# Seven-product down projections over both column halves, kept in two PSUM banks

## The chip, the cores and the metric

The kernel runs on one core of a Trainium2 chip. The metric is the device time of one execution in microseconds, the median of several runs. The engines are named PE or TensorE (matmuls), ACT or ScalarE, DVE or VectorE, POOL or GpSimd, and SP, whose queue only issues transfers here.

## The reference, cut to what matters

A decoder trunk of two layers works on 256 tokens of width 2048 in float32. Each layer adds a mixer to the residual (layer 0: windowed attention and a state-space scan, layer 1: dilated attention) and then an MLP. The change touches the MLPs alone, with D_FF = 8192:

```
def squared_relu_mlp(h, w_up, w_down):
    u = jnp.einsum('bsd,df->bsf', h, w_up)
    return jnp.einsum('bsf,fd->bsd', jnp.square(jax.nn.relu(u)), w_down)
...
        h = rms_norm(x, norm_ffn[layer])
        x = x + squared_relu_mlp(h, w_up[layer], w_down[layer])
```

## The kernel before, in words

Products are made with split numbers: every float32 operand becomes a high part (hi, a copy by ScalarE to float32r) and a low part (lo, the difference, by VectorE). A product of two such operands is three matmuls: hi x hi, hi x lo and lo x hi.

All matmul work stands in one list, `plan` (line 219 on), of pieces. A piece covers two k-tiles of 128 rows (KC = 2) and 512 weight columns, so one weight tile of 128x1024 and 512 KB. A piece of a `Unit` makes 12 matmuls: 2 k-tiles x 2 token halves x 3. `run` (line 270) walks the list and, while it issues piece i, runs ahead of it: the weight load of piece i + 6 on SP's queue (`fetch`), the hi copy of piece i + 3 (`high`, ScalarE), the lo subtraction of piece i + 2 (`low`, VectorE), and any weight sum of piece i + 4 (`add`, VectorE). The buffers are 4 loaded tiles (wraw), 5 of hi and 4 of lo. Each engine works through its instructions in the order in which they were issued.

Work beside the matmuls (norms, attention, activations, splits) is written as generators; `side` queues them, and `tick` (line 173), called once per k-tile or once per seven-product piece, lets them issue some steps when ScalarE and VectorE are not too far ahead by an estimate of their load. `need` forces them on until a label is done.

An MLP has 16 up units of 512 columns (8 pieces each) and 8 chunks c of two up results. After an up unit, `squared` (line 929) runs relu, 8 transposes through PSUM (tile uT) and Square. `operands` (line 948) then splits the results of a chunk into uh and ul and, in all chunks but the last, forms four sums of activations s1 and s2 and splits them into sh and sl; it starts when the chunk before has issued all its products. `down` (line 983) is the usual down unit: one chunk's 8 k-tiles times 512 columns, 4 pieces, added to a stripe of the residual `res` by VectorE.

`Seven` (line 243) takes the place of two down units. With tokens in two halves, a chunk's rows in two and the columns in two, the product of a 2x2 block matrix of activations and one of weights needs 7 block products instead of 8 (a scheme after Strassen and Winograd): 7 products x 2 pieces x 6 matmuls = 84 instead of 96. In exchange, sums of weight blocks and of activation blocks are needed. Before the change this is done for column stripes 0 and 1 of chunks 0 to 6 in each layer; stripes 2 and 3 and all of chunk 7 go through `down`. The weight blocks (tile sraw) are 128x1024 tiles in a pool of 29 slots with the tag w4, which many other tiles share; four of the seven weight operands are sums made by VectorE. Each product has a PSUM bank of its own (tile sp, from the four aux banks that transposes use too). `evict` (line 995) adds it to the residual, or, for P1, Q5 and Q6, to running sums in SBUF that `together` (line 1009) combines into the residual once per layer; the first two stripes of chunk 7 wait for that (`pre`).

The order of a chunk: up, two down units, up, with the 14 seven-product pieces spread between them from place 4.5 on.

Of the kernel before, what the change touches and what calls it, by code (L numbers as in the profile page):

```python
# [11 lines left out]
OP = mybir.AluOpType  # L12
# [28 lines left out]
def trunk(ctx: ExitStack, tc: tile.TileContext, x, norm_mix, norm_ffn, w_up, w_down, ab_w_in, ab_q_norm,  # L41
# [193 lines left out]
    def unit(*a, **k):  # L235
# [4 lines left out]
    SEVEN = (("P1", "11", None), ("P2", "21", None), ("Q3", "22", None), ("Q5", "11", "12"), ("Q7", "12", "22"),  # L240
             ("Q6", "11", "22"), ("Q4", "11", "21"))

    class Seven:


        def __init__(self, w, rows, c0, kts, operands, evict, needs, mark):
            self.w, self.rows, self.c0, self.operands, self.evict, self.needs, self.mark = \
                w, rows, c0, operands, evict, needs, mark
            self.halves = kts // KC
            self.raw = {}  # L250
            self.pieces = [(self, (p, h)) for p in range(7) for h in range(self.halves)]

        def fetch(self, p, h):
            _, block, other = SEVEN[p]
            b = block if other is None else "12" if p == 3 else None
            if b is not None:
                r, c = self.rows[int(b[0]) - 1] + h * KC, self.c0 + (int(b[1]) - 1) * W
                self.raw[b, h] = t = work.tile([128, KC, W], F32, name="sraw", tag="w4")
                nc.sync.dma_start(t, self.w[r * 128:(r + KC) * 128, c:c + W].rearrange("(k p) c -> p k c", p=128))

        def add(self, p, h):
            _, block, other = SEVEN[p]
            if other is not None:
                t = self.raw[block, h]
                V.tensor_tensor(t, t, self.raw[other, h], op=OP.add)

        def source(self, p, h):
            return self.raw[SEVEN[p][1], h]

    def run():  # L270
# [32 lines left out]
        def low(i):  # L303
            if i < len(todo):
# [3 lines left out]
                parts[i].append(lo)  # L308

# [15 lines left out]
        before = ps = sp = None  # L325
        kept, held = [], []
        for i, (u, c) in enumerate(todo):
# [9 lines left out]
            if isinstance(u, Seven):  # L337
                p, h = c
                name = SEVEN[p][0]
                if p in u.needs and h == 0:  # L340
                    need(u.needs[p])
                if h == 0:
                    sp = aux("sp")
                xh, xl, t0 = u.operands(name)
                tick(True)
                for k in range(KC):
                    q = h * KC + k
                    wh, wl = xh[:, q, t0:t0 + 128], xl[:, q, t0:t0 + 128]
# [249 lines left out]
    def residual_unit(w, ktiles, j, needs={}, nm=None, last=None, pre=None, mark=None):  # L598
# [557 lines left out]
```

## Time and profile before

| | |
|---|---|
| median of 3 runs | 2298.36 us (2297.48 to 2298.86) |
| the profiled execution's own time | 2297.73 us |
| its span | 2295.9 us |
| granted TensorE clock, mean | 0.998 |
| busy: PE, DVE, ACT | 2277.0, 1692.5, 1239.9 us |
| matmuls of 512 columns in seven-product pieces (sp) | 1176 |
| matmuls of 512 columns in down units (acc on uh, ul) | 1728 |
| weight sums by VectorE (sraw<-sraw) | 112 |
| HBM read | 420.64 MB |

The span is the time from the first to the last instruction of the profiled execution; its own time is that of the whole launch. A busy TensorE says only that a matmul was under way: matmuls overlap, so their pace is read from the starts of neighbouring ones. A group's last figure is the idle time of the engine just before its instructions, with what ended it. "PE acc" is a matmul into an accumulator of a unit, "PE sp" one into a bank of the seven products; whi and wlo are the weights' hi and lo, hThi and hTlo those of the normed input, uh and ul those of the up result, and sh and sl those of its sums.

### The profile page before, as it was taken

What the parts mean: (1) busy time and instruction counts of PE and PEld (TensorE: products, weight loads), DVE (VectorE), ACT (ScalarE), POOL (GpSimd) and SP (SyncE); (2) the same over time, 40 slices, a digit from 0 to 9 for tenths busy, and PEclk for the clock granted to TensorE, in tenths of its full rate; (3) what the DMA queues carried; (4) which work ended last, traced back from release to release, by engine and by line L of the source; (5) the groups of instructions that cost most, each with busy time, mean ns of one, the idle gap of its engine ahead of it and who ended that gap; (6) DMA issues with size and microseconds to landing.
All of it is one profiled execution on the core that took longest, in us unless ns stands there. A gap on an engine that the chain in (4) does not pass through costs nothing.

```text
span 2295.9 us, 29951 instructions
## 1 busy us (share of the span) xinstructions
PE 2277.0 (99%) x11149; PEld 1898.3 (83%) x11149; DVE 1692.5 (74%) x2418; ACT 1239.9 (54%) x1561; POOL 8.4 (0%) x20
## 2 busy tenths in 40 slices
PE   8999999999999999999999999999999999999998
PEld 7998988888888888888788778778888888888887
DVE  6779976556787787787866766665577787787785
ACT  5565554445556556556454555555555555555553
POOL 1000000000000000000000000000000000000000
PEclk9999999999999999999999999999999999999999
DMA  7546565566556656656456455545756656656654
GB/s 232 166 139 193 174 186 173 191 186 222 187 176 223 187 177 222 188 177 222 145 177 190 148 162 160 173 156 178 221 163 217 206 164 217 205 164 218 204 165 145
DMA packets 229202, 424.73 MB, mean 185 GB/s; under 512 B 15620, under 2 KB 26160, under 8 KB 229056
## 3 DMA queue, kind: packets, MB, share of 16 engines
q1 hardware_dynamic: 218976, 416.34, 58.1%
q10 hardware_dynamic: 9568, 6.34, 0.9%
q8 instruction: 87, 1.43, 0.2%
q14 instruction: 59, 0.48, 0.1%
q0 software_dynamic: 512, 0.15, 0.0%
HBM read 420.64 MB, written 2.13 MB: 184 GB/s over the span
## 4 chain that ended last, share of the span: by engine, by line
PE 98%; DVE 1%; DMA 0%; ACT 0%; issue 0%; SPq 0%; ACTq 0%
PE acc L71 81%; PE sp L71 12%; PE uT L71 1%; PE sc L71 1%; PE o L71 1%; PE pT L71 1%; PE yp L71 1%; PE xT L71 1%; DMA wraw<-in_ab_w_in_dram 0%; DVE res L71 0%; PE qp L71 0%; DVE wlo L71 0%; PE yo L71 0%; PE kp L71 0%; PE yT L71 0%; PE xtok L71 0%
## 5 line engine op out<-in xcount | busy, mean ns | idle before, releaser
L71 ACT ACTIVATE whi<-wraw 128x1024 fp32r<-128x1024 f32 (+1 forms) x680 | 717.4, 1056 | 641.4 <-PE acc L71 518.1
L71 DVE TENSOR_TENSOR wlo<-wraw,whi 128x1024 fp32r<-128x1024 f32 (+1 forms) x680 | 823.4, 1216 | 314.7 <-PE acc L71 227.5
L71 PE MATMUL acc<-whi,hThi 128*128 128x512 f32 (+1 forms) x1632 | 645.5, 396 | 2.6 <-ACT hThi L71 2.6
L71 PE MATMUL acc<-whi,hTlo 128*128 128x512 f32 (+1 forms) x1632 | 634.7, 389 | 0.3 <-DVE hTlo L71 0.3
L71 PE MATMUL acc<-wlo,hThi 128*128 128x512 f32 (+1 forms) x1632 | 633.9, 388 | 0.0
L71 PEld LDWEIGHTS acc<-whi,hThi 128*128 128x128 f32 x1632 | 307.6, 189 | 68.1 <-issue 5.9
L71 PEld LDWEIGHTS acc<-whi,hTlo 128*128 128x128 f32 x1632 | 307.3, 188 | 64.7 <-DVE hTlo L71 0.9
L71 PEld LDWEIGHTS acc<-wlo,hThi 128*128 128x128 f32 x1632 | 307.8, 189 | 60.4 <-issue 1.0
L71 ACT ACTIVATE whi<-sraw 128x1024 fp32r<-128x1024 f32 x196 | 207.7, 1060 | 178.4 <-DVE sraw L71 151.1
L71 DVE TENSOR_TENSOR wlo<-sraw,whi 128x1024 fp32r<-128x1024 f32 x196 | 239.7, 1223 | 59.4 <-PE acc L71 30.4
L71 PE MATMUL acc<-whi,uh 128*128 128x512 f32 x576 | 228.7, 397 | 3.4 <-ACT uh L71 3.4
L71 PE MATMUL acc<-whi,ul 128*128 128x512 f32 x576 | 226.0, 392 | 1.7 <-DVE ul L71 1.7
L71 PE MATMUL acc<-wlo,uh 128*128 128x512 f32 x576 | 225.5, 391 | 0.0
L71 DVE TENSOR_TENSOR sraw<-sraw 128x1024 f32<-128x1024 f32 x112 | 136.6, 1220 | 0.0
L71 PEld LDWEIGHTS acc<-whi,ul 128*128 128x128 f32 x576 | 108.9, 189 | 25.7 <-DVE ul L71 2.6
L71 PEld LDWEIGHTS acc<-whi,uh 128*128 128x128 f32 x576 | 108.9, 189 | 25.4 <-ACT uh L71 3.8
L71 PEld LDWEIGHTS acc<-wlo,uh 128*128 128x128 f32 x576 | 109.0, 189 | 21.7
L71 PE MATMUL acc<-hThi,whi 128*128 128x256 f32 x384 | 112.3, 293 | 0.0
L71 PE MATMUL acc<-hThi,wlo 128*128 128x256 f32 x384 | 108.5, 283 | 0.0
L71 PE MATMUL acc<-hTlo,whi 128*128 128x256 f32 x384 | 108.5, 283 | 0.0
L71 PE MATMUL sp<-whi,sh 128*128 128x512 f32 x224 | 87.1, 389 | 0.0
L71 PE MATMUL sp<-wlo,sh 128*128 128x512 f32 x224 | 87.1, 389 | 0.0
(228 smaller groups left out, 2535.9 us busy)
## 6 DMA issues: line engine op xcount, KB each, us to landing
wraw<-in_w_up_dram SPq DMA_DIRECT2D x256, 512.0 KB, 3.7
wraw<-in_w_down_dram SPq DMA_DIRECT2D x144, 512.0 KB, 4.3
sraw<-in_w_down_dram SPq DMA_DIRECT2D x112, 512.0 KB, 5.9
wraw<-in_ab_w_in_dram SPq DMA_DIRECT2D x96, 512.0 KB, 3.7
wraw<-in_c_w_qkv_dram SPq DMA_DIRECT2D x96, 512.0 KB, 4.0
wraw<-in_ab_w_out_dram SPq DMA_DIRECT2D x48, 512.0 KB, 3.7
wraw<-in_c_w_o_dram SPq DMA_DIRECT2D x32, 512.0 KB, 3.7
wt<-cumd ACTq DMA_DIRECT2D x8, 512.0 KB, 6.5
```

The costliest lines, as they stand in the source:

```text
L71: return f(out, *a, **k)
```

## The change

- `Seven` is made for a column offset: `seven(c, j)` for stripes j and j + 1. Chunks 0, 2 and 4 of each layer use it for both halves (j = 0 and j = 2) and have no down units; chunks 1, 3, 5 and 6 use it for stripes 0 and 1 as before. That is 20 sets in place of 14.
- Up units come in another order: 3 in the chunks with both halves, 1 in the chunks 1, 3 and 5, and units 14 and 15 at the head of chunk 6 with the two down units behind them.
- The seven products of a set go to two long-lived PSUM banks (a: P1, Q6, Q5, Q3; c: Q7, Q4) and a third for P2. A bank is not cleared between its products; after each product VectorE adds or subtracts the bank's running sum to or from one block of the residual. The running sums in SBUF, `together` and the wait `pre` are gone.
- Of the four weight sums, one (block 11 + block 12) is made by a transfer issued from GpSimd that reads block 12 from HBM and adds it to the tile of block 11 (`accum_op`); it is issued behind P1's lo subtraction, which reads that tile. The other three stay on VectorE, Q6's with a tile of its own (t2). The three loads of blocks 21, 12 and 22 are issued together with P2.
- The sums of activations have the opposite sign: two of the four operations become scalar_tensor_tensor.
- `operands` waits for all products of the chunk before, and for chunk 7 only for the up result.

```
```diff
@@ -237,35 +237,55 @@
-    SEVEN = (("P1", "11", None), ("P2", "21", None), ("Q3", "22", None), ("Q5", "11", "12"), ("Q7", "12", "22"),
-             ("Q6", "11", "22"), ("Q4", "11", "21"))
+    SEVEN = (("P1", "a", "11"), ("P2", "b", "21"), ("Q6", "a", "t2"), ("Q7", "c", "12"), ("Q5", "a", "11"),
+             ("Q4", "c", "21"), ("Q3", "a", "22"))
+    LOADS = {"P1": ("11",), "P2": ("21", "12", "22")}
+    SUMS = {"Q6": ("t2", "11", "22"), "Q7": ("12", "12", "22"), "Q4": ("21", "21", "t2")}
     class Seven:
-        def __init__(self, w, rows, c0, kts, operands, evict, needs, mark):
-            self.w, self.rows, self.c0, self.operands, self.evict, self.needs, self.mark = \
-                w, rows, c0, operands, evict, needs, mark
+        def __init__(self, w, rows, c0, kts, operands, to, needs, mark):
+            self.w, self.rows, self.c0, self.operands, self.to, self.needs, self.mark = \
+                w, rows, c0, operands, to, needs, mark
             self.halves = kts // KC
-            self.raw = {}
+            self.raw, self.bank = {}, {}
             self.pieces = [(self, (p, h)) for p in range(7) for h in range(self.halves)]
+        def tile(self, b, h):
+            self.raw[b, h] = t = work.tile([128, KC, W], F32, name="sraw", tag="w4")
+            return t
         def fetch(self, p, h):
-            _, block, other = SEVEN[p]
-            b = block if other is None else "12" if p == 3 else None
-            if b is not None:
+            for b in LOADS.get(SEVEN[p][0], ()):
                 r, c = self.rows[int(b[0]) - 1] + h * KC, self.c0 + (int(b[1]) - 1) * W
-                self.raw[b, h] = t = work.tile([128, KC, W], F32, name="sraw", tag="w4")
-                nc.sync.dma_start(t, self.w[r * 128:(r + KC) * 128, c:c + W].rearrange("(k p) c -> p k c", p=128))
+                nc.sync.dma_start(self.tile(b, h),
+                                  self.w[r * 128:(r + KC) * 128, c:c + W].rearrange("(k p) c -> p k c", p=128))
         def add(self, p, h):
-            _, block, other = SEVEN[p]
-            if other is not None:
-                t = self.raw[block, h]
-                V.tensor_tensor(t, t, self.raw[other, h], op=OP.add)
+            if SEVEN[p][0] in SUMS:
+                o, x, y = SUMS[SEVEN[p][0]]
+                x, y = self.raw[x, h], self.raw[y, h]
+                V.tensor_tensor(self.raw[o, h] if o != "t2" else self.tile(o, h), x, y, op=OP.add)
+        def accumulate(self, p, h):
+            if SEVEN[p][0] == "P1":
+                r, c = self.rows[0] + h * KC, self.c0 + W
+                nc.gpsimd.dma_start(self.raw["11", h],
+                                    self.w[r * 128:(r + KC) * 128, c:c + W].rearrange("(k p) c -> p k c", p=128),
+                                    accum_op=OP.add)
         def source(self, p, h):
-            return self.raw[SEVEN[p][1], h]
+            return self.raw[SEVEN[p][2], h]
+        def evict(self, p):
+            name, b, _ = SEVEN[p]
+            t, j, op = {"P1": (0, 0, OP.add), "P2": (0, 0, OP.add), "Q6": (1, 0, OP.add), "Q7": (1, 1, OP.subtract),
+                        "Q5": (1, 1, OP.subtract), "Q4": (1, 0, OP.add), "Q3": (0, 1, OP.subtract)}[name]
+            r = self.to[t][j]
+            V.tensor_tensor(r, r, self.bank[b], op=op)
     def run():
         todo = plan
@@ -306,6 +326,9 @@
                 lo = wpool.tile([128, KC, raw.shape[2]], F32R, name="wlo", bufs=AHEAD + 1)
                 V.tensor_tensor(lo, raw, f32(parts[i][0]), op=OP.subtract)
                 parts[i].append(lo)
+                u, c = todo[i]
+                if isinstance(u, Seven):
+                    u.accumulate(*c)
         for i in range(RAW):
             if i % 2 == 0:
@@ -336,21 +359,23 @@
             hi, lo = parts.pop(i)
             if isinstance(u, Seven):
                 p, h = c
-                name = SEVEN[p][0]
+                name, b, _ = SEVEN[p]
                 if p in u.needs and h == 0:
                     need(u.needs[p])
-                if h == 0:
-                    sp = aux("sp")
+                new = b not in u.bank
+                if new:
+                    u.bank[b] = aux("sp")
+                sp = u.bank[b]
                 xh, xl, t0 = u.operands(name)
                 tick(True)
                 for k in range(KC):
                     q = h * KC + k
                     wh, wl = xh[:, q, t0:t0 + 128], xl[:, q, t0:t0 + 128]
-                    PE.matmul(sp, wh, hi[:, k], start=q == 0, stop=False)
-                    PE.matmul(sp, wh, lo[:, k], start=False, stop=False)
-                    PE.matmul(sp, wl, hi[:, k], start=False, stop=q == u.halves * KC - 1)
+                    PE.matmul(sp, wh, hi[:, k], start=new and k == 0, stop=False, skip_group_check=True)
+                    PE.matmul(sp, wh, lo[:, k], start=False, stop=False, skip_group_check=True)
+                    PE.matmul(sp, wl, hi[:, k], start=False, stop=q == u.halves * KC - 1, skip_group_check=True)
                 if h == u.halves - 1:
-                    pending.append(lambda u=u, name=name, sp=sp: u.evict(name, sp))
+                    pending.append(lambda u=u, p=p: u.evict(p))
                     if p == 6:
                         done.add(u.mark)
                 continue
@@ -947,9 +970,11 @@
         def operands(c):
-            if c:
-                yield from until(("seven", layer, c - 1))
-                yield from until(("rest", layer, c - 1))
+            if 0 < c < NC - 1:
+                for k in marks[c - 1]:
+                    yield from until(k)
+            if c == NC - 1:
+                yield from until(("uf", layer, 2 * c + 1))
             for i in (2 * c, 2 * c + 1):
                 yield from until(("uf", layer, i))
                 u[i] = slot("uh"), slot("ul")
@@ -961,10 +986,10 @@
             a1, a2 = uf[2 * c], uf[2 * c + 1]
             s1, s2 = w4([128, 4, T], "s1"), w4([128, 4, T], "s2")
             o, n = slice(0, 128), slice(128, T)
-            V.tensor_tensor(s1[:, :, o], a1[:, :, n], a2[:, :, n], op=OP.subtract)
-            V.tensor_tensor(s1[:, :, n], a1[:, :, o], s1[:, :, o], op=OP.subtract)
-            V.tensor_tensor(s2[:, :, o], a1[:, :, n], a1[:, :, o], op=OP.subtract)
-            V.tensor_tensor(s2[:, :, n], a2[:, :, o], s1[:, :, n], op=OP.subtract)
+            V.tensor_tensor(s1[:, :, o], a2[:, :, n], a1[:, :, n], op=OP.subtract)
+            V.scalar_tensor_tensor(s1[:, :, n], a1[:, :, o], -1.0, s1[:, :, o], op0=OP.mult, op1=OP.subtract)
+            V.tensor_tensor(s2[:, :, o], a1[:, :, o], a1[:, :, n], op=OP.subtract)
+            V.scalar_tensor_tensor(s2[:, :, n], a2[:, :, o], -1.0, s1[:, :, n], op0=OP.mult, op1=OP.subtract)
             yield 2
             sums[c] = [(slot("sh"), slot("sl")) for _ in range(2)]
             for (h, l), s in zip(sums[c], (s1, s2)):
@@ -980,63 +1005,44 @@
             return Unit([(wu, i * W, W)], nm.ktiles(), lambda ps: after_up(i, ps),
                         needs=nm.needs() if i == 0 else {}).pieces
+        marks = {c: [] for c in range(NC)}
         def down(c, j):
             kts = [(4 * (2 * c + b) + k, (lambda b=b, k=k: u[2 * c + b] + (k,))) for b in range(2) for k in range(4)]
             end = c == NC - 1
+            marks[c].append(("down", layer, c, j))
             return residual_unit(wd, kts, j, {4 * b: ("u", layer, 2 * c + b) for b in range(2)},
-                                 nxt if end else None, last if end else None,
-                                 ("seven's sums", layer) if end and j < 2 else None,
-                                 ("rest", layer, c) if j == NS - 1 else None).pieces
...
-        def seven(c):
+                                 nxt if end else None, last if end else None, marks[c][-1]).pieces
+        def seven(c, j):
             def parts(name):
                 i, k, t = {"P1": (0, 0, 0), "P2": (0, 1, 0), "Q4": (0, 1, 128), "Q5": (1, 0, 0), "Q6": (1, 0, 128),
                            "Q7": (1, 1, 0), "Q3": (1, 1, 128)}[name]
                 return (sums[c][k] if i else u[2 * c + k]) + (t,)
-            return Seven(wd, (8 * c, 8 * c + 4), 0, 4, parts, lambda name, ps: evict(c, name, ps),
+            marks[c].append(("down", layer, c, j))
+            return Seven(wd, (8 * c, 8 * c + 4), j * W, 4, parts,
+                         [[res[:, t, (j + i) * W:(j + i + 1) * W] for i in range(2)] for t in range(2)],
                          {0: ("u", layer, 2 * c), 1: ("u", layer, 2 * c + 1), 2: ("sums", layer, c)},
-                         ("seven", layer, c)).pieces
+                         marks[c][-1]).pieces
+        def mixed(rest, s, start):
+            n, k = len(s), 0
+            for i, x in enumerate(rest):
+                while k < n and i >= start + (len(rest) - start) / n * k:
+                    plan.append(s[k])
+                    k += 1
+                plan.append(x)
+            plan.extend(s[k:])
         plan.extend(up(0) + up(1))
-        for c in range(NC - 1):
-            rest = up(2 * c + 2) + down(c, 2) + down(c, 3) + up(2 * c + 3)
-            s = seven(c)
-            for k, x in enumerate(rest):
-                while s and k >= 4.5 + (len(rest) - 4.5) / 14 * (14 - len(s)):
-                    plan.append(s.pop(0))
-                plan.append(x)
-            plan.extend(s)
+        for c, (ups, both) in enumerate((((2, 3, 4), 1), ((5,), 0), ((6, 7, 8), 1), ((9,), 0), ((10, 11, 12), 1),
+                                         ((13,), 0), ((14, 15), 0))):
+            p = [up(i) for i in ups]
+            d = [] if both else [down(c, 2), down(c, 3)]
+            order = p[:1] + d + p[1:] if c < NC - 2 else p + d
+            mixed(sum(order, []), seven(c, 0) + (seven(c, 2) if both else []), 4.5)
         for j in range(NS):
             plan.extend(down(NC - 1, j))
```

## Rows read from the trace of the kernel before

**Rows 1.** The page, part 1: busy time and share of the span, by engine.
```profile
PE 2277.0 (99%) x11149; PEld 1898.3 (83%) x11149; DVE 1692.5 (74%) x2418; ACT 1239.9 (54%) x1561; POOL 8.4 (0%) x20
```

**Rows 2.** The page, part 4: the chain that ended last, by engine.
```profile
PE 98%; DVE 1%; DMA 0%; ACT 0%; issue 0%; SPq 0%; ACTq 0%
```

**Rows 3.** The chain in order of time: start us, length us, what, matmuls.
```profile
725.83 5.44 PE acc L71 x24
...
812.04 5.44 PE acc L71 x24
```

**Rows 4.** The page, part 5: one group of the seven products' matmuls.
```profile
L71 PE MATMUL sp<-whi,sh 128*128 128x512 f32 x224 | 87.1, 389 | 0.0
```

**Rows 5.** Timeline of TensorE at both layers' ends: start us, us, what, [idle before].
```profile
1136.52 0.39 PE L71 MATMUL acc<-whi,hTlo 128*128 128x512 f32 x1
...
1140.36 0.50 PE L71 MATMUL acc<-whi,uh 128*128 128x512 f32 x1 [1.68 <-ACT uh L71]
...
1143.40 0.63 PE L71 MATMUL acc<-whi,ul 128*128 128x512 f32 x1
1143.83 0.63 PE L71 MATMUL acc<-whi,uh 128*128 128x512 f32 x1
...
1145.09 0.39 PE L71 MATMUL acc<-whi,uh 128*128 128x512 f32 x1
...
2241.86 0.39 PE L71 MATMUL acc<-whi,hTlo 128*128 128x512 f32 x1
...
2251.04 0.39 PE L71 MATMUL acc<-whi,ul 128*128 128x512 f32 x1
```

**Rows 6.** Timeline of ScalarE at the end of layer 0's MLP.
```profile
1136.27 1.37 ACT L71 ACTIVATE relu<-acc,rs 128x512 f32<-128x512 f32 x2 [0.98 <-PE acc L71]
...
1139.24 2.01 ACT L71 ACTIVATE uh<-uf 128x1024 fp32r<-128x1024 f32 x2
```

**Rows 7.** The page, part 5: groups of VectorE (count, busy us, mean ns).
```profile
L71 DVE TENSOR_TENSOR wlo<-sraw,whi 128x1024 fp32r<-128x1024 f32 x196 | 239.7, 1223 | 59.4 <-PE acc L71 30.4 <-issue 24.8
...
L71 DVE TENSOR_TENSOR sraw<-sraw 128x1024 f32<-128x1024 f32 x112 | 136.6, 1220 | 0.0
...
L71 DVE TENSOR_TENSOR res<-sp,res 128x512 f32<-128x512 f32 x56 | 38.6, 690 | 10.8 <-PE sp L71 9.2
```

**Rows 8.** Timeline of VectorE where its operations follow one another.
```profile
845.28 1.22 DVE L71 TENSOR_TENSOR sraw<-sraw 128x1024 f32<-128x1024 f32 x1
846.42 0.69 DVE L71 TENSOR_TENSOR pq<-sp,pq 128x512 f32<-128x512 f32 x1
847.02 1.22 DVE L71 TENSOR_TENSOR wlo<-wraw,whi 128x1024 fp32r<-128x1024 f32 x1
```

**Rows 9.** Stretches: length, busy us by engine, clock, DMA share, GB/s.
```profile
718.00:804.00 86.00, 86.00 (x389) 71.23 (x388) 67.79 (x66) 47.97 (x51) 0.00 (x0) 1.00 0.63 195
798.00:804.00 6.00, 6.00 (x30) 4.99 (x29) 4.06 (x5) 3.64 (x5) 0.00 (x0) 1.00 0.95 323
920.00:940.00 20.00, 20.00 (x90) 16.57 (x89) 18.54 (x19) 10.15 (x10) 0.00 (x0) 1.00 0.46 133
```

**Rows 10.** Timeline of GpSimd: one issue of a 16 KB transfer.
```profile
8.97 0.56 POOL L124 DMA_DIRECT2D dtb<-in_ab_dt_bias_dram  x1
```

**Rows 11.** DMA issues: transfer, queue, count, KB each, median us to landing.
```profile
sraw<-in_w_down_dram SPq DMA_DIRECT2D x112, 512.0 KB, 5.9
...
par<-in_norm_mix_dram ACTq DMA_DIRECT2D x1, 16.0 KB, 2.1
...
dtb<-in_ab_dt_bias_dram POOLq DMA_DIRECT2D x1, 16.0 KB, 5.2
```

**Rows 12.** The tile wraw: landing of its 512 KB loads.
```profile
DMA to landing us min/median/max: 3.4/3.8/9.6
```

**Rows 13.** Waits of VectorE and of SP's queue: us in total, times, longest us.
```profile
DVE wlo L71 <- PE acc L71: 257.9, 186, 3.0
...
SPq L285 <- DVE wlo L71: 1813.0, 629, 7.8
```

More of the change, by code (lines that the diff above doesn't have):

```diff
@@ L324, in run @@
         pending = []
-        before = ps = sp = None
+        before = ps = None
         kept, held = [], []
@@ L596, in add_stripe, with residual_unit @@
         free(ps)
-    def residual_unit(w, ktiles, j, needs={}, nm=None, last=None, pre=None, mark=None):
+    def residual_unit(w, ktiles, j, needs={}, nm=None, last=None, mark=None):
         def after(ps):
-            if pre is not None:
-                need(pre)
             add_stripe(ps, j, last)
@@ L985, in down @@
             end = c == NC - 1
+            marks[c].append(("down", layer, c, j))
             return residual_unit(wd, kts, j, {4 * b: ("u", layer, 2 * c + b) for b in range(2)},
-                                 nxt if end else None, last if end else None,
-                                 ("seven's sums", layer) if end and j < 2 else None,
-                                 ("rest", layer, c) if j == NS - 1 else None).pieces
-        keep = {}
-        R = [[res[:, t, j * W:(j + 1) * W] for j in range(2)] for t in range(2)]
-        def evict(c, name, ps):
-            if c == 0 and name == "P1":
-                keep["pq"], keep["q6"] = w4([128, 2, W], "pq"), w4([128, W], "q6")
-                keep["P1"], keep["Q5"], keep["Q6"] = keep["pq"][:, 0], keep["pq"][:, 1], keep["q6"]
-                V.tensor_tensor(R[1][0], R[1][0], R[1][1], op=OP.add)
-            if name in keep and c == 0:
-                S.activation(keep[name], ps, AF.Copy)
-            else:
-                r = {"P2": R[0][0], "Q3": R[0][1], "Q4": R[1][0], "Q7": R[1][1]}.get(name)
-                r = keep[name] if r is None else r
-                V.tensor_tensor(r, ps, r, op=OP.add)
-            if c == NC - 2 and name == "Q4":
-                side(together(), ("seven's sums", layer))
-        def together():
-            P1, Q5, Q6 = keep["P1"], keep["Q5"], keep["Q6"]
-            V.tensor_tensor(R[0][0], P1, R[0][0], op=OP.add)
-            V.tensor_tensor(P1, Q6, P1, op=OP.subtract)
-            V.tensor_tensor(R[1][1], P1, R[1][1], op=OP.add)
-            V.tensor_tensor(R[1][0], R[1][0], R[1][1], op=OP.subtract)
-            yield 2
-            V.tensor_tensor(P1, P1, Q5, op=OP.add)
-            V.tensor_tensor(R[0][1], P1, R[0][1], op=OP.add)
-            V.tensor_tensor(R[1][1], Q5, R[1][1], op=OP.add)
-            yield 1
-        def seven(c):
+                                 nxt if end else None, last if end else None, marks[c][-1]).pieces
+        def seven(c, j):
             def parts(name):
```

## The prediction, made before the kernel was run

> **What bounds the kernel now.** I read the page's busy table first, then the chain of waits, then TensorE's own timeline where the chain breaks. TensorE is busy 2277.0 of 2295.9 us and carries 98% of the chain that ended last [rows 1, 2], so time is won by taking matmuls away or by closing TensorE's few gaps, and lost where another engine opens new ones. The chain in order of time gives the price of a matmul: 24 of them in 5.44 us, 0.2267 us each [rows 3]; the 389 ns that the groups show [rows 4] is the length of one, and they overlap. The two rows of [rows 3] stand at the same place of two neighbouring chunks, 812.04 - 725.83 = 86.21 us apart. A chunk has 2 x 96 matmuls of up, 2 x 48 of down and 84 of the seven products: 372 x 0.2267 = 84.33 us. The other 1.88 us are its 16 uT transposes, 0.118 us each. So inside the layer TensorE has no gap at all; VectorE and ScalarE wait for it.
>
> The gaps are at the end of each MLP. There the chunk's last up unit is followed at once by the down unit that needs its result: relu, transposes, Square, the split, and then matmuls that first run at half pace [rows 5, 6].
>
> **Part 1, fewer matmuls.** Chunks 0, 2 and 4 of both layers replace two down units (96 matmuls) by one more set of seven products (84). That is 6 sets x 12 = 72 matmuls of 128x512, 72 x 0.2267 = 16.3 us, all on the path, since TensorE sets the pace there. Weight loads go with the matmuls and transposes stay the same. Both bounds of this term are near: TensorE can't gain more than 16.3 here, and what it can lose is in the parts below.
>
> **Part 2, the last up units earlier.** In chunk 6 the order becomes up 14, up 15, down, down, so eight down pieces (8 x 12 x 0.2267 = 21.8 us) and about half of the seven products lie between the end of up 15 and the first matmul of chunk 7. The chain to be hidden is short: from the last up matmul at 1136.52 to the first down matmul at 1140.36 [rows 5, 6]. What it costs today: in layer 0 the tenth down matmul starts at 1145.09, the first after which the pace is 0.23 us again. Without a gap it would start 0.227 us (the last up matmul) + 0.94 us (8 transposes) + 9 x 0.2267 us after 1136.52, at 1139.73: 5.4 us lost. In layer 1 the twelfth starts at 2251.04 and would have started at 2241.86 + 0.23 + 0.94 + 11 x 0.2267 = 2245.52: 5.5 us. The part behind the gap is TensorE's clock: matmuls 0.43 us apart instead of 0.23, after an idle engine; no gap, no slow matmuls. I take the whole 10.9 us. If another 2 us gap took its place, most of the slow stretch would come back with it, and the term would be near 0.
> The final combination (8 additions of VectorE per layer and the wait for them ahead of the first two stripes) goes too. It lies beside this same chain and is not priced again.
>
> **Part 3, what VectorE gets.** Each piece of the seven products needs a hi copy on ScalarE and a lo subtraction on VectorE for only 6 matmuls (1.36 us), where another piece has 12 (2.72 us). VectorE's 128x1024 operations take 1.22 us each, but follow one another every 1.13 to 1.14 us, and the 512-column ones every 0.60 us [rows 7, 8].
> A chunk with both halves: 52 pieces, 12 weight sums, 2 ul, 2 sl, so 68 x 1.14 = 77.5 us, and 14 evictions and 4 sums of activations, 18 x 0.6 = 10.8: 88 us. TensorE takes 456 x 0.2267 + 24 x 0.118 = 106.2 us for it. A chunk with one half: 40 x 1.14 + 15 x 0.6 = 54.6 us against 276 x 0.2267 + 0.94 = 63.5. So 83 and 86%; before, it is 67.8 of 86 us [rows 9]. Locally it is tighter. From Q6 to Q4 in a one-half chunk there are 8 + 5 pieces, 24.5 us of TensorE, with 13 subtractions, 6 sums, 4 evictions and 2 stripes: 19 x 1.14 + 6 x 0.6 = 25.3 us, 0.8 us too much. TensorE always has about three pieces ready, 4 to 7 us, which covers it; the trace already has stretches of 18.5 in 20 us without a gap on TensorE [rows 9]. I cost this at 0; if every operation took its full 1.22 us it would be 2.4 us of backlog, still covered.
> The evictions now go straight into the residual (0.69 us, the same row as before), and a bank's next product comes two pieces after its eviction, so TensorE doesn't wait for it. Two scalar-tensor-tensor operations replace two subtractions in each chunk, at the same size: 0 to 0.06 us each on VectorE (hidden).
>
> **Part 4, the accumulating DMA.** New for the trace: 40 transfers (20 sets x 2) of 512 KB issued by GpSimd, each behind the lo subtraction of P1 on the same tile, each awaited by VectorE's sum for Q6. GpSimd has nothing else to do in this stretch, its issue takes about 0.56 us [rows 10], and SP's queue is not passed. Behind the waiting sum on VectorE stand the lo subtractions of the next pieces, and TensorE waits for those.
> The time there is: lo has 4 buffers, so VectorE does P1's lo when TensorE has finished the piece four places ahead, and Q6's sum comes after the lo two places ahead of it in the same way. Between these two TensorE works through five pieces, which by their order are 9.5 to 12.2 us, in one case four pieces, 8.2 us. If the sum is late, TensorE still has four pieces ready, 6.8 to 8.2 us; less the three 1.14 us operations that VectorE has to do in them, 3.4 to 4.7 us are to spare. So TensorE starves only if issue to landing takes longer than about 13 us (12.9 to 15.6 by place).
> How long it takes is bounded from rows [rows 11, 12]. From below: a 16 KB transfer from GpSimd lands after 5.2 us, one from ACT after 2.1, and the fastest 512 KB load after 3.4, so 5.2 + (3.4 - 2.1) = 6.5 us. From above: twice the slowest 512 KB load and GpSimd's extra 3.1, 2 x 9.6 + 3.1 = 22.3 us. I take 5.2 + (5.9 - 2.1) = 9.0 us, since the median load of the same tile is the nearest row. That is inside the time there is: 0 us.
> At the upper end each set would stall TensorE for 22.3 - 14 = 8.3 us, 20 x 8.3 = 166 us.
> The Trainium skill, Collectives: The Full Stack, section "The bandwidth ceiling: the fold count and why AG ≠ RS ≠ AR", says that an add inside a DMA needs two source reads and so ran at about half the rate of a copy. By that rule the estimate would be 5.2 + 2 x 3.8 = 12.8 us, which still adds nothing to the sum but uses up the margin. No run here shows such a transfer yet.
> Other DMA traffic: three loads of a half are now issued together at P2, six within about 4 to 7 us, with one or two other loads, some 3.7 MB. At the 323 GB/s that a busy stretch moves [rows 9] they take 11 us, and SP runs ahead by four other pieces (about 18 us in the dense part), because its waits are for lo on the other pieces' buffers [rows 13]. In total there are as many loads as before (48 fewer wraw, 48 more sraw) and 21 MB more from the accumulating ones, 5% of 420 MB. Cost 0; without SP's lead, ScalarE would wait 1 to 3 us in each set.
>
> **Sum.** 2297.73 (the profiled execution's own time; the median of the runs is 0.6 above) - 16.3 - 10.9 = 2270.5 us, and 2271.1 against the median. Prediction 2271.
>
> **Rivals.**
> (a) The transfer or VectorE eats the margin. A landing near 13 us makes VectorE wait 1 to 4 us for both halves, on top of the 0.8 us backlog, and TensorE loses 0.3 to 1 us in each of 20 sets: 6 to 20 us, 2277 to 2291. For it: 83 to 86% load on one engine, and in-order queues in which one wait delays the rest. Against it: VectorE waits for TensorE in the trace, 257.9 us in all for lo alone [rows 13].
> (b) Slower than before: the accumulating transfer takes over 15.5 us from issue to landing. Then each set loses more than 1.4 us, and 20 x 1.4 = 28 us is more than the gain of 27.2. At 16 us it is 20 x 2 = 40 us, about 2311. For it: one load took 9.6 us, and twice that is over the limit. Against it: the median load takes 5.9.
> (c) Only the matmuls count: the reordering leaves a gap at the layer's end (the operands of chunk 7 split late, or the wait moves to another tile), 2297.73 - 16.3 = 2281.4, 2282 against the median. Against it: about 30 us lie between, and the split needs 4 us.
>
> **How the numbers follow.** Forecast (2267 to 2276): 0.58. (a): 0.20. (b): 0.11. (c): 0.06. An end within 0.2% (4.6 us, about what a measurement of this kernel can tell from no change), by (a) and (b) cancelling the gain: 0.05. So faster 0.84, same 0.05, slower 0.11. The range 2267 to 2289 leaves out (b), the cancelled case and the top of (a), and its lower end is 4 us under the sum for prices read a little low.
>
> **What would show it.** Right: sp matmuls 1680 instead of 1176, acc matmuls on u 1152 instead of 1728; the wait for uh and ul by TensorE gone; a pair of chunks with up units 2 to 5 lasting 169.7 us instead of 172.4; the GpSimd transfers landing in under 13 us and VectorE's wait for them under 2 us each. Wrong: waits of TensorE for whi or wlo tied to sraw in each set, landings over 15 us, or a granted clock under full inside the MLP.

## The result and the profile after

The changed kernel takes 2275.08 us (median of 4 runs, 2274.05 to 2276.79) against 2298.09 (2297.48 to 2298.86): ratio 0.990, 95% interval 0.9883 to 0.9918, 23.0 us less. The forecast was 2271, in a range of 2267 to 2289. The profiled execution took 2276.79 us with a span of 2274.1; it is the slowest of the four, 1.7 us over their median, so a gap that stands in its trace need not stand in the others.

The page of the changed kernel, parts 1 and 4 (busy time by engine, then the chain that ended last), which answer to [rows 1, 2]:

```profile
PE 2258.5 (99%) x11077; PEld 1881.3 (83%) x11077; DVE 1744.0 (77%) x2470; ACT 1266.6 (56%) x1591; POOL 56.6 (2%) x60
...
PE 95%; DMA 2%; ACT 1%; DVE 1%; issue 1%; SPq 0%; POOL 0%; ACTq 0%; POOLq 0%; DVEq 0%
```

72 instructions of TensorE are gone, and its busy time is 18.5 us shorter. It still carries the chain, but 95% of it instead of 98%: some of the path now runs over other engines.

The groups of the changed kernel, from the view by line (count, then busy us and mean ns, then idle before); they answer to [rows 4, 7]:

```profile
L71 PE MATMUL acc<-whi,uh 128*128 128x512 f32 x384 | 151.5, 394 | 0.0
...
L71 PE MATMUL sp<-whi,sh 128*128 128x512 f32 x320 | 124.5, 389 | 0.0
...
L71 PE MATMUL sp<-whi,uh 128*128 128x512 f32 x240 | 93.4, 389 | 0.0
...
L71 DVE TENSOR_TENSOR wlo<-sraw,whi 128x1024 fp32r<-128x1024 f32 x280 | 341.3, 1221 | 83.5 <-PE acc L71 63.3 <-issue 13.4 <-ACT whi L71 2.5
...
L71 DVE TENSOR_TENSOR sraw<-sraw 128x1024 f32<-128x1024 f32 x120 | 146.3, 1219 | 11.9 <-DMA sraw<-in_w_down_dram 11.9
...
L71 DVE TENSOR_TENSOR res<-res,sp 128x512 f32<-128x512 f32 x140 | 95.5, 682 | 13.4 <-PE sp L71 13.4
```

Each matmul group stands for three of one size: 3 x (320 + 240) = 1680 on sp and 3 x 384 = 1152 on acc with u, as the prediction counted. The durations are those of before. New is the idle time ahead of VectorE's weight sums.

Transfers of the changed kernel (queue, count, KB each, median us to landing), against [rows 11]:

```profile
sraw<-in_w_down_dram SPq DMA_DIRECT2D x160, 512.0 KB, 8.2
...
sraw<-in_w_down_dram POOLq DMA_DIRECT2D x40, 512.0 KB, 9.5
```

The 40 accumulating transfers land after 9.5 us (median; 11.4 at the longest). SP's plain loads of the same tile went from 5.9 to 8.2 us.

Waits of the changed kernel, over the whole span (us in total, times, longest us), against [rows 13]:

```profile
ACT whi L71 <- DVE sraw L71: 139.2, 86, 3.3
...
ACT whi L71 <- DMA wraw<-in_w_up_dram: 31.8, 15, 6.0
...
DVE sraw L71 <- DMA sraw<-in_w_down_dram: 11.9, 13, 1.4
...
PE uT L71 <- ACT relu L71: 2.6, 7, 1.2
...
PE acc L71 <- DVE wlo L71: 0.5, 2, 0.3
```

TensorE's waits for uh and ul are gone, and so is the gap of [rows 5]. VectorE's wait for the accumulating transfers is 1.4 us at most. But TensorE now waits seven times for relu, inside the MLP, where it had no gap before, and ScalarE has a wait for up weights that the waits of before don't list. ScalarE's wait for VectorE's sums is not new; only its longest grew. Before:

```profile
ACT whi L71 <- DVE sraw L71: 151.1, 96, 2.3
```

What is new is where relu stands: before, none of the 32 relus comes right behind a hi copy that waited for such a sum; after, 18 do.

I summed, over TensorE's timeline of most of the two MLPs and their ends (600 to 1150 and 1520 to 2255 us), what lies from one start to the next beyond 0.2268 us for each 512-column matmul and 0.118 for each transpose. Before it is 5.1 + 5.2 us, at the layers' ends. After it is 1.3 + 4.1, and nothing of it stands there: 2.1 us are five gaps of 0.3 to 0.5 us in front of transposes whose relu came behind a hi copy that waited 2.0 us for a sum of VectorE, 1.9 us one place where the hi copies ahead of relu waited for loads, and 1.1 us three gaps in front of late low parts. These few microseconds are what the forecast missed.

ScalarE's timeline at the first of these places in the changed kernel (start us, length us, what, idle before):

```profile
731.59 1.07 ACT L71 ACTIVATE whi<-sraw 128x1024 fp32r<-128x1024 f32 x1 [1.56 <-DVE sraw L71]
732.55 1.04 ACT L71 ACTIVATE whi<-wraw 128x1024 fp32r<-128x1024 f32 x1
735.59 1.06 ACT L71 ACTIVATE whi<-sraw 128x1024 fp32r<-128x1024 f32 x1 [1.99 <-DVE sraw L71]
736.56 1.24 ACT L71 ACTIVATE relu<-acc,rs 128x512 f32<-128x512 f32 x2
```

And TensorE's there:

```profile
737.28 0.33 PE L71 MATMUL uT<-cst,relu 128*128 128x128 f32 x1
737.86 0.55 PE L71 MATMUL uT<-cst,relu 128*128 128x128 f32 x3 [0.25 <-ACT relu L71]
```

ScalarE sits idle for 2 us although relu's input is complete, because the instruction ahead of relu is a hi copy that waits for a weight sum of VectorE. Then relu comes too late for its transposes. The largest such place, after up unit 14 in chunk 6 of layer 1:

```profile
2157.11 1.06 ACT L71 ACTIVATE whi<-wraw 128x1024 fp32r<-128x1024 f32 x1 [2.30 <-DMA wraw<-in_w_up_dram]
2161.08 1.06 ACT L71 ACTIVATE whi<-sraw 128x1024 fp32r<-128x1024 f32 x1 [2.90 <-DMA sraw<-in_w_down_dram]
2166.93 1.06 ACT L71 ACTIVATE whi<-wraw 128x1024 fp32r<-128x1024 f32 x1 [4.79 <-DMA wraw<-in_w_up_dram]
...
2169.20 1.25 ACT L71 ACTIVATE relu<-acc,rs 128x512 f32<-128x512 f32 x2
```

Here the hi copies wait for loads, six of sraw having been issued from 2142.61 on, three together. TensorE's timeline has a gap of 1.4 us and one of 0.46 where it waits for this relu. At the same place of layer 0 it has none.

### The profile page after: what moved, and what is told of

It reads as the page before. It is cut to its first block, busy times and chain, and to the rows that moved or that the text cites. A ratio compares the mean times of both kernels' runs of the same rounds, so it can differ in the third digit from the quotient of the medians.

```text
span 2274.1 us, 30081 instructions
## 1 busy us (share of the span) xinstructions
PE 2258.5 (99%) x11077; PEld 1881.3 (83%) x11077; DVE 1744.0 (77%) x2470; ACT 1266.6 (56%) x1591; POOL 56.6 (2%) x60
## 3 DMA queue, kind: packets, MB, share of 16 engines
q1 hardware_dynamic: 218976, 416.34, 57.1%
q0 software_dynamic: 11392, 21.12, 5.2%
## 4 chain that ended last, share of the span: by engine, by line
PE 95%; DMA 2%; ACT 1%; DVE 1%; issue 1%; SPq 0%; POOL 0%; ACTq 0%; POOLq 0%; DVEq 0%
PE acc L71 74%; PE sp L71 15%; PE uT L71 1%; PE sc L71 1%; PE o L71 1%; PE pT L71 1%; DMA sraw<-in_w_down_dram 1%; DMA wraw<-in_w_up_dram 1%; PE yp L71 1%; PE xT L71 0%; DMA wraw<-in_ab_w_in_dram 0%; ACT relu L71 0%; DVE wlo L71 0%; ACT whi L71 0%; PE qp L71 0%
## 5 line engine op out<-in xcount | busy, mean ns | idle before, releaser
L71 ACT ACTIVATE whi<-wraw 128x1024 fp32r<-128x1024 f32 (+1 forms) x632 | 666.2, 1055 | 610.7 <-PE acc L71 434.3
L71 DVE TENSOR_TENSOR wlo<-wraw,whi 128x1024 fp32r<-128x1024 f32 (+1 forms) x632 | 765.0, 1215 | 264.7 <-PE acc L71 183.8
L71 PE MATMUL acc<-whi,hThi 128*128 128x512 f32 (+1 forms) x1632 | 646.9, 396 | 2.0 <-ACT hThi L71 2.0
L71 PE MATMUL acc<-whi,hTlo 128*128 128x512 f32 (+1 forms) x1632 | 634.7, 389 | 0.9 <-DVE hTlo L71 0.9
L71 PE MATMUL acc<-wlo,hThi 128*128 128x512 f32 (+1 forms) x1632 | 634.0, 388 | 0.6 <-DVE wlo L71 0.5
L71 ACT ACTIVATE whi<-sraw 128x1024 fp32r<-128x1024 f32 x280 | 296.3, 1060 | 212.8 <-DVE sraw L71 139.2
L71 DVE TENSOR_TENSOR wlo<-sraw,whi 128x1024 fp32r<-128x1024 f32 x280 | 341.3, 1221 | 83.5 <-PE acc L71 63.3
L71 PEld LDWEIGHTS acc<-whi,hThi 128*128 128x128 f32 x1632 | 307.3, 188 | 67.2 <-issue 5.8
L71 PEld LDWEIGHTS acc<-whi,hTlo 128*128 128x128 f32 x1632 | 307.0, 188 | 65.7 <-DVE hTlo L71 1.8
L71 PEld LDWEIGHTS acc<-wlo,hThi 128*128 128x128 f32 x1632 | 307.5, 188 | 61.9 <-DVE wlo L71 1.9
L71 DVE TENSOR_TENSOR sraw<-sraw 128x1024 f32<-128x1024 f32 x120 | 146.3, 1219 | 11.9 <-DMA sraw<-in_w_down_dram 11.9
L71 PE MATMUL acc<-whi,uh 128*128 128x512 f32 x384 | 151.5, 394 | 0.0
L71 PE MATMUL acc<-whi,ul 128*128 128x512 f32 x384 | 149.7, 390 | 0.0
L71 PE MATMUL acc<-wlo,uh 128*128 128x512 f32 x384 | 149.5, 389 | 0.0
L71 PE MATMUL sp<-whi,sl 128*128 128x512 f32 x320 | 124.6, 389 | 0.0
L71 PE MATMUL sp<-whi,sh 128*128 128x512 f32 x320 | 124.5, 389 | 0.0
L71 PE MATMUL sp<-wlo,sh 128*128 128x512 f32 x320 | 124.5, 389 | 0.0
L71 PE MATMUL acc<-hThi,whi 128*128 128x256 f32 x384 | 112.4, 293 | 0.0
L71 PE MATMUL acc<-hThi,wlo 128*128 128x256 f32 x384 | 108.6, 283 | 0.0
L71 PE MATMUL acc<-hTlo,whi 128*128 128x256 f32 x384 | 108.6, 283 | 0.0
L71 DVE TENSOR_TENSOR res<-res,sp 128x512 f32<-128x512 f32 x140 | 95.5, 682 | 13.4 <-PE sp L71 13.4
L275 POOL DMA_DIRECT2D sraw<-in_w_down_dram x40 | 48.2, 1204 | 2094.9 <-DVE wlo L71 1655.4
## 6 DMA issues: line engine op xcount, KB each, us to landing
wraw<-in_w_up_dram SPq DMA_DIRECT2D x256, 512.0 KB, 4.3
sraw<-in_w_down_dram SPq DMA_DIRECT2D x160, 512.0 KB, 8.2
wraw<-in_ab_w_in_dram SPq DMA_DIRECT2D x96, 512.0 KB, 3.7
wraw<-in_w_down_dram SPq DMA_DIRECT2D x96, 512.0 KB, 4.0
wraw<-in_c_w_qkv_dram SPq DMA_DIRECT2D x96, 512.0 KB, 3.9
wraw<-in_ab_w_out_dram SPq DMA_DIRECT2D x48, 512.0 KB, 3.7
sraw<-in_w_down_dram POOLq DMA_DIRECT2D x40, 512.0 KB, 9.5
wraw<-in_c_w_o_dram SPq DMA_DIRECT2D x32, 512.0 KB, 3.6
```

The lines of the kernel that those rows point to most:

```text
L71: return f(out, *a, **k)
L275: nc.gpsimd.dma_start(self.raw["11", h], self.w[r * 128:(r + KC) * 128, c:c + W].rearrange("(k p) c -> p k c", p=128), accum_op=OP.add)
```

## The experiments

All were run with repeated timing beside the kernel before, whose median lay between 2297.6 and 2298.3 us each time; "against after" is against 2275.08.

### One part undone at a time

**e1_no_accum**: the accumulating transfer is left out, VectorE makes the sum.

```diff
         def add(self, p, h):
+            if SEVEN[p][0] == "Q6":
+                V.tensor_tensor(self.raw["11", h], self.raw["11", h], self.raw["12", h], op=OP.add)
...
-                    u.accumulate(*c)
```

> The sum of blocks 11 and 12 goes back to VectorE (40 more sums of 1.14 us), no accumulating DMA. Theory (the 4 us short of the forecast come from transfers: the loads issued together at P2, and the accumulating transfer beside them): 21 MB less traffic, the loads at P2 stay, part of the gaps goes, 2272 to 2275 us. Rival (VectorE's load of 83 to 86% makes the gaps): 46 us more on VectorE, 2278 to 2290 us.

Measured 2283.13 us, ratio 0.9936 (0.9924 to 0.9949): 8.0 us slower than after. The waits of this run:

```profile
ACT whi L71 <- DVE sraw L71: 200.2, 104, 4.0
...
PE acc L71 <- DVE wlo L71: 4.3, 6, 1.1
...
ACT whi L71 <- DMA wraw<-in_w_up_dram: 3.9, 4, 1.7
...
PE uT L71 <- ACT relu L71: 1.5, 6, 0.2
```

And its two chunks from 643 to 814 us (length; busy us of PE, PEld, DVE, ACT, POOL; clock, DMA share, GB/s), then the same of the changed kernel:

```profile
643.00:814.00 171.00, 170.17 (x764) 140.06 (x763) 152.87 (x148) 100.55 (x106) 0.00 (x0) 1.00 0.60 196
```

```profile
643.00:814.00 171.00, 170.75 (x771) 141.18 (x770) 147.34 (x142) 102.18 (x107) 7.19 (x6) 1.00 0.70 217
```

40 sums of 1.22 us more, VectorE at 89% of the stretch instead of 86%, and TensorE begins to wait for low parts, while its waits for relu do not grow. So the theory of the expectation is out, VectorE was not as free as I had it, and the accumulating transfer earns its place, though it adds 10 points of DMA share. It has a price that this run shows too: without the accumulating transfers, and with the three loads still together, ScalarE waits 3.9 us for up weights instead of 31.8.

**e3_old_end**: the old order of the last up units.

```diff
-            order = p[:1] + d + p[1:] if c < NC - 2 else p + d
+            order = p[:1] + d + p[1:]
```

> Chunk 6 in the old order (up, down, down, up), all else as changed. By the prediction's step the gap at each layer's end comes back: 2275 + 10.9 = 2286 us. Rival (the reordering is worth little, since the final combination was what delayed the end): 2276 to 2280 us.

Measured 2284.39 us, 0.9943 (0.9931 to 0.9956): 9.3 us slower than after, the term of 10.9 a little smaller. TensorE's timeline shows the gap of [rows 5] back, and the slow matmuls behind it:

```profile
1131.05 0.98 PE L71 MATMUL uT<-cst,relu 128*128 128x128 f32 x7 [0.35 <-ACT relu L71]
1133.71 0.79 PE L71 MATMUL acc<-whi,uh 128*128 128x512 f32 x1 [1.68 <-ACT uh L71]
```

**e4_one_half**: the products for one column half in every chunk, the rest of the change kept.

```diff
-        for c, (ups, both) in enumerate((((2, 3, 4), 1), ((5,), 0), ((6, 7, 8), 1), ((9,), 0), ((10, 11, 12), 1),
-                                         ((13,), 0), ((14, 15), 0))):
+        for c, (ups, both) in enumerate((((2, 3), 0), ((4, 5), 0), ((6, 7), 0), ((8, 9), 0), ((10, 11), 0),
+                                         ((12, 13), 0), ((14, 15), 0))):
```

> 14 sets of seven products as before, with the banks, the accumulating DMA and the late order of chunk 6 as changed; up units two to a chunk. By the prediction's steps only the matmul term goes: 2275 + 16.3 = 2291 us. If the six added sets cost gaps of 4 us in all, these go too: 2287 us. Rival (the gaps come from the accumulating DMA in each set, so 14/20 of them stay): 2290 us.

Measured 2286.36 us, 0.9950 (0.9937 to 0.9964), 11.7 less than before. By my sum TensorE loses under 1 us in its MLPs. So the end term is 9.3 (taken away from after) to 11.7 (added to before), around the 10.9 of the forecast; the 11.7 is not the order of the units alone, since the banks, the accumulating transfers and the missing final combination are in it too. And the six added sets gave 11.3 us instead of 16.3: this is where 5 us went.

**e2_spread**: two loads at P1 and two at P2 instead of one and three.

```diff
-    LOADS = {"P1": ("11",), "P2": ("21", "12", "22")}
+    LOADS = {"P1": ("11", "22"), "P2": ("21", "12")}
```

> Block 22 is loaded with P1 instead of P2, so two loads and two loads instead of one and three; nothing else changes. Theory (loads issued together): ScalarE's wait for wraw loads (31.8 us) and TensorE's gaps shrink, 2271 to 2273 us. Rival (VectorE, or the accumulating transfer alone): as the changed kernel, 2274 to 2276 us.

Measured 2273.70 us (2273.22 to 2274.15), 0.9896 (0.9882 to 0.9909). It is 1.4 us under after, at the edge of what runs that overlap can tell, and between the two ranges of the expectation. ScalarE's wait for up weights falls from 31.8 to 18.1 us, and the gap of 1.4 us at 2168 is gone from the trace; TensorE still waits for relu, for 0.2 us each time:

```profile
PE uT L71 <- ACT relu L71: 1.3, 6, 0.2
```

### The place of relu

**e11_relu_only**: on ScalarE, relu is issued as soon as its up unit is complete, without waiting for a `tick`, and ahead of the next hi copy. By the same edit VectorE's evictions are issued ahead of the next weight sum.

```diff
             if i:
                 low(i + AHEAD - 1)
                 fetch(i + AHEAD - 1 + RAW)
-                high(i + AHEAD)
-                add(i + AHEAD + 1)
             for f in pending:
                 f()
             pending = []
+            if i:
+                high(i + AHEAD)
+                add(i + AHEAD + 1)
...
         def after_up(i, ps):
-            side(squared(i, ps), ("uf", layer, i))
+            g = squared(i, ps)
+            if ("rs", nm.row) in done:
+                tasks.append([clock[0] + next(g), g, ("uf", layer, i)])
+            else:
+                side(g, ("uf", layer, i))
```

> The changed kernel with only the relu issued ahead of the high copy, the three loads still together at P2. If the relu's place is the main cause of the lost 5 us: 2271.0 to 2272.0 (the spread alone gave 1.4 us, both together 5.1). If both causes only work together, so that late loads still stall ScalarE: 2273 to 2275.

Measured 2270.66 us (2269.93 to 2272.17), 0.9879 (0.9866 to 0.9893): 4.4 us under after. ScalarE at the place shown above for the changed kernel (TensorE's matmuls stand within 0.1 us of each other in the two):

```profile
729.01 1.04 ACT L71 ACTIVATE whi<-wraw 128x1024 fp32r<-128x1024 f32 x1
729.99 1.37 ACT L71 ACTIVATE relu<-acc,rs 128x512 f32<-128x512 f32 x2
732.19 1.06 ACT L71 ACTIVATE whi<-sraw 128x1024 fp32r<-128x1024 f32 x1 [0.83 <-DVE sraw L71]
```

relu runs 6.6 us earlier, and the hi copy that waits for VectorE is behind it. The sum of TensorE's gaps falls from 1.3 + 4.1 to -0.2 - 0.3 us, which is none within the error of the unit prices; TensorE's waits no longer list relu. ScalarE still waits 154.0 us for weight sums and 25.6 us for up weights; at 20 sets that costs nothing once no relu stands behind. The other half of the edit, the evictions, can't be what shortened relu's wait: it puts the sums later, and ScalarE's wait for them grew, from 139.2 us to the 154.0. Whether it had a part in the end of the three gaps for low parts (1.1 us) is not shown.

**e6_relu_first**: the same with the loads spread as in e2_spread.

> Loads two and two, and the relu of an up unit is issued on ScalarE ahead of the hi copy of the piece three places on, not behind it. Theory (what is left of the gaps, 3 us, is the relu standing behind a hi copy that waits for VectorE's weight sum): 2271 us. Rival (relu first only moves the wait to the hi copy): 2273 to 2275 us.

Measured 2270.01 us (2269.67 to 2270.14), 0.9877 (0.9863 to 0.9890), the fastest median of all runs, 5.1 us under after and 28 under before. Against e11_relu_only the spread no longer gives anything that can be told.

**e5_two_accum**: e2_spread with Q7's sum made by a second accumulating transfer. **e7_two_accum_relu**: the same with relu first.

```diff
-    SUMS = {"Q6": ("t2", "11", "22"), "Q7": ("12", "12", "22"), "Q4": ("21", "21", "t2")}
+    SUMS = {"Q6": ("t2", "11", "22"), "Q4": ("21", "21", "t2")}
+    MORE = {"P1": ("11", 0, 1), "P2": ("12", 1, 1)}
```

The rest of the edit makes `accumulate` issue one transfer for each entry of `MORE`.

> Loads two and two (as the run that spreads them), and a second weight sum (12 + 22) by accumulating DMA: 40 sums of 1.14 us fewer on VectorE, 40 more transfers of 512 KB. Theory (VectorE's sums are what holds ScalarE's copies, and the relu behind them, so less of them means fewer gaps): 2271 to 2273 us. Rival (transfers: 21 MB more and one more burst): 2275 to 2280 us.

> Both of the above at once. Theory: no gap is left in the MLPs, 2270 to 2271 us. Rival (the second accumulating transfer crowds the loads): 2274 to 2280 us.

Measured 2272.67 us, 0.9890 (0.9876 to 0.9903), and 2270.16 us, 0.9877 (0.9864 to 0.9891). Without relu first, less work on VectorE gives 1 us against e2_spread, which is not clear of noise (the runs overlap); with it, nothing. So with relu first, at 20 sets, neither VectorE nor the transfers hold TensorE any more.

### How far it can be taken

Each further chunk with both halves (a dense chunk) takes 12 matmuls away in each layer. With relu first and the loads spread I added some: one chunk more in each layer (22 sets), or three (26), with one accumulating transfer per set and half or two. If TensorE stayed the bound, 22 sets would give 2270.0 - 24 x 0.2267 = 2264.6 us, and 26 sets 2253.7.

```diff
-                                         ((13,), 0), ((14, 15), 0))):
+                                         ((13, 14), 1), ((15,), 0))):
```

That is 22 sets; for 26 the groups (5, 6), (7, 8), (9, 10) and (11, 12) stand with both halves between (2, 3, 4) and (13, 14).

> As the run before, with both column halves in 6 of 8 chunks (two up units in each), 26 sets instead of 20: 72 matmuls fewer, 16.3 us. If TensorE stays the bound: 2255 us. VectorE would have 75 of 83.5 us in such a chunk (89%), and the transfers some 21 MB in it (250 GB/s before the second reads of the accumulating ones). If the gaps grow as in the run without accumulating DMA (VectorE at 91%, 8 us): 2260 to 2266 us. If the transfers are the bound: over 2270 us.

> The dense version (both halves in 6 of 8 chunks, 26 sets) with one accumulating transfer per set instead of two; VectorE makes Q7's sum again, 52 additions of 1.22 us (63 us) more than in the dense version with two. If TensorE were the bound: 2270.0 - 16.3 = 2254. If the landings of the accumulating transfers made the dense version 2300, half of them gone takes most of the stalls with them: 2255 to 2285. If VectorE's load did it (86% of the window there, 92% here): 2300 to 2320.

> The best version (one accumulating transfer, loads spread, relu ahead of the high copy) with both halves in a fourth chunk of each MLP: 22 sets instead of 20, 24 matmuls of 0.2267 us fewer = 5.4 us. If TensorE stays the bound: 2264.6 (2263 to 2266). If the sixth chunk already has no room beside VectorE and the transfers: 2268 to 2280.

> Four of 8 chunks with both halves as in the run with 22 sets (2275.0 us; VectorE 90.4% busy at 1000 to 1100 us, TensorE 3.1 us idle there), and Q7's sum too by an accumulating transfer, 44 additions of 1.22 us less on VectorE. If VectorE's load in two dense chunks in a row holds the sixth chunk: its share there falls to about 85% and the time to 2264.6 to 2268. If the transfers do it (44 more of them): 2275 to 2282.

| run | sets | accumulating transfers per set and half | us | ratio (95%) | over TensorE's bound |
|---|---|---|---|---|---|
| e6_relu_first | 20 | 1 | 2270.01 | 0.9877 (0.9863 to 0.9890) | 0 |
| e12_four_two | 22 | 2 | 2270.12 | 0.9877 (0.9860 to 0.9893) | 5.5 |
| e10_four | 22 | 1 | 2274.99 | 0.9896 (0.9880 to 0.9911) | 10.4 |
| e8_dense | 26 | 2 | 2300.23 | 1.0009 (1.0000 to 1.0018) | 46.5 |
| e9_dense_one | 26 | 1 | 2314.29 | 1.0067 (1.0054 to 1.0079) | 60.6 |

None of the four with more sets reached the bound, my expectation for 26 sets (2255) missed by 45 us, and e12_four_two fell between the two ranges that I had given it. The windows from 1000 to 1100 us, where the sixth chunk is dense in all but the first, in the order of the table:

```profile
1000.00:1100.00 100.00, 100.00 (x453) 82.85 (x451) 80.63 (x78) 57.31 (x61) 2.41 (x2) 1.00 0.63 198
```

```profile
1000.00:1100.00 100.00, 97.11 (x433) 78.79 (x433) 85.39 (x84) 61.06 (x67) 9.79 (x8) 1.00 0.86 241
```

```profile
1000.00:1100.00 100.00, 96.93 (x429) 77.86 (x429) 90.39 (x88) 60.80 (x66) 4.85 (x4) 1.00 0.68 208
```

```profile
1000.00:1100.00 100.00, 97.03 (x429) 78.51 (x429) 85.59 (x84) 60.18 (x64) 14.67 (x12) 1.00 0.86 252
```

```profile
1000.00:1100.00 100.00, 95.97 (x426) 77.22 (x425) 90.36 (x90) 60.42 (x66) 6.05 (x5) 1.00 0.73 230
```

Two or more dense chunks in a row bring TensorE 3 to 4 us of gaps per 100. With one transfer VectorE is at 90%; with two it is at 85%, and the DMA share goes from about 0.7 to 0.86. Taking sums off VectorE was faster at both counts, by 4.9 and 14.1 us, in spite of 44 and 52 more transfers. So VectorE's load is a limit here, and weighs more than the added transfers. What holds back the 5.5 us that e12_four_two is still over the bound, with VectorE at 85%, is not settled.

In e8_dense TensorE waits for low parts, and VectorE ahead of them for its accumulating transfers:

```profile
DVE sraw L71 <- DMA sraw<-in_w_down_dram: 79.5, 33, 5.5
...
PE sp L71 <- DVE wlo L71: 18.2, 21, 2.0
```

In the changed kernel the first of these is 11.9 us. How much of the 46.5 us is landing and how much is VectorE's work I did not separate.

## Why the prediction was right, and where it was not

The time lies 4 us over the forecast and inside its range; the direction and the two large terms came out as worked out.

- **Part 1, 16.3 us.** Right as a price: from one half everywhere to the changed plan with relu first is 2286.36 - 2270.66 = 15.7 us (e4_one_half, which loses next to nothing by gaps, to e11_relu_only). The change itself got 11.3 of it.
- **Part 2, 10.9 us.** Measured 9.3 and 11.7 from its two sides. No 2 us gap took the place of the old one. The windows at layer 0's end, of the changed kernel and then of e3_old_end (the number after POOL is the granted clock):

```profile
1120.00:1150.00 30.00, 30.00 (x138) 24.85 (x137) 19.64 (x21) 14.47 (x18) 0.00 (x0) 1.00 0.63 194
```

```profile
1130.00:1140.00 10.00, 7.83 (x24) 5.36 (x23) 4.22 (x4) 5.27 (x8) 0.00 (x0) 0.66 0.35 117
```

  Full clock without a gap, and 0.66 of it where the old order idles TensorE.
- **Part 4, the landing.** Estimated 9.0 us, measured 9.5 (median). VectorE's waits were forecast under 2 us each and are 1.4 at most, so the margin was there. That the two figures are so close is luck: the plain load in the sum rose from 5.9 to 8.2 us, with which the same sum gives 11.3, and GpSimd's transfer takes 1.3 us longer than that load, not the 3.1 of [rows 11]. By the rule of two source reads (the Trainium skill, Collectives: The Full Stack, section "The bandwidth ceiling: the fold count and why AG ≠ RS ≠ AR") the estimate was 12.8 us; no transfer of the changed kernel took that long. But the rule, which the page gives for the ReduceScatter of a ring, is one of rate, and the time of the DMA engines agrees with it. Part 3 of the changed kernel's page gives packets, MB and share of the 16 engines for SP's loads (q1) and GpSimd's transfers (q0, all but 0.15 MB of them accumulating):

```profile
q1 hardware_dynamic: 218976, 416.34, 57.1%
q0 software_dynamic: 11392, 21.12, 5.2%
```

  Per MB that is 0.25% against 0.14%, 1.8 times as much, where two reads for one would be up to twice. Whether the add or GpSimd's queue makes it, no run separates.
- **The step that failed: "Other DMA traffic ... Cost 0; without SP's lead, ScalarE would wait 1 to 3 us in each set", with the cost of 0 in Part 3.** It cost 4.4 us (e11_relu_only) to 5.1 (e6_relu_first). Both steps asked whether TensorE would run out of ready pieces, and it hardly did (0.5 us of waits for low parts, 1.1 by the starts of its matmuls). They left out what else stands in ScalarE's queue. relu is behind the hi copies; a hi copy waits up to 3.3 us for VectorE's sum, or 6.0 us for an up load; and the transposes, which have a fixed place among TensorE's matmuls, find relu late. In e11_relu_only relu goes ahead of the copies, 4.4 us come back, and TensorE's gaps go. In the trace 2.1 us belong to the zero of Part 3 (copies waiting for sums) and 1.9 to that of the transfers (copies waiting for loads). The late loads come with the accumulating transfers: the wait for up weights is 31.8 us, 18.1 with the loads spread (e2_spread), 4.8 with relu first as well (e6_relu_first), and 3.9 without those transfers though the loads stand together (e1_no_accum). Whether the three loads together make the gap of the 1.9 us is not shown: e2_spread lacks it, but e5_two_accum, with the loads spread as well, has it again, with 1.06 us, and e1_no_accum, with the loads together, lacks it.
- **A pair of chunks, forecast 169.7 us instead of 172.4.** The chain of the changed kernel in order of time:

```profile
643.49 8.20 PE acc L71 x36
...
813.74 8.20 PE acc L71 x36
...
984.46 8.20 PE acc L71 x36
```

  170.25 and 170.72 us: 0.55 and 1.0 us too long. The gaps of this kind in them are 0.46 us at 737, and 0.29 and 0.45 us at 903 and 908.
- **Rivals.** (a), a loss at every set that takes the time to 2277 to 2291, has the right sign, but not the place: TensorE didn't wait for late landings. Its picture of in-order queues was the right one, on the wrong engine. (b) is out: in the changed kernel no transfer took over 11.4 us to land, and VectorE waits 11.9 us for them in all. (c) is out: TensorE has no gap at the layers' ends, and the old order costs 9.3 us (e3_old_end). That VectorE's load was closer to its limit than the "0" of Part 3 sounds is shown by e1_no_accum: 8.0 us from 40 sums more.

## What to carry to other kernels

When you cost added work at nothing because the bounding engine has pieces in hand, go through the queue of every engine that prepares them, and ask which short instruction with a fixed due time stands behind one that can now wait: here a relu behind a copy. Issuing the short one first cost nothing here and got back all that was lost. Before putting more on an engine at 85% in one stretch, take the load away or add it in one run: 40 operations more cost 8 us here, and the next dense chunk gave nothing, with a second accumulating transfer, or cost 5 us without it.

## What the runs showed of the hardware that I had not expected

- One issue of an accumulating 512 KB transfer keeps GpSimd 1.20 us (48.2 us for 40), where its 16 KB transfer took 0.56 [rows 10]. With two per set and half, and 26 sets, the mean of the 104 issues is 1.61 us and the median landing 11.1 us.
- A single gap does not always bring slow matmuls. After the 1.4 us gap at 2168 in the changed kernel the next matmuls start 0.23 us apart, with a granted clock of 1.00 from 2165 to 2180; in e3_old_end a gap of 1.68 us with another of 0.35 ahead of it took the clock of its 10 us to 0.66, with 0.50, the lower of the two levels (1.2 GHz), from 1134 to 1140. Two cases make no rule.
- Landings of plain loads grow where several are issued together: the same 512 KB load of sraw from SP took 5.9 us (median) before, when each was issued by itself, and 8.2 after. The accumulating transfers are not the cause: without them it is 8.3 (e1_no_accum), and with the loads two and two 8.6 (e2_spread).
- An accumulating transfer takes 1.8 times as much of the DMA engines' time per MB as the plain loads beside it (5.2% for 21.12 MB against 57.1% for 416.34).
